# Staging tiles of a decoder trunk: six instead of four in the pair stages, moved to the right end of SBUF behind an empty margin

## The chip, the cores and the metric

The kernel runs on one core of a Trainium2 chip. The time is that of one execution on the device in microseconds; the profile is one further execution, taken by the hardware profiler.

## The reference

The reference is one layer of a hybrid decoder on 256 rows of width 4096, in float32. After an RMSNorm a wide projection W_in gives the inputs of two token mixers (gated linear attention with a per-channel decay; sliding-window attention with sinks) and of two merge gates. Each mixer's result is projected back to 4096 columns, both are merged by sigmoid gates, an output projection and a residual add follow, and a last RMSNorm:

```python
h = rms_norm(x, norm_gains[l])
z = h @ w_in[l]
...
y_a = (o_a * jax.nn.silu(gg)) @ w_gla_out[l]
...
y_b = (o_b * jax.nn.silu(sg)) @ w_swa_out[l]
merged = jax.nn.sigmoid(ga + b_gates[l, 0]) * y_a + jax.nn.sigmoid(gb + b_gates[l, 1]) * y_b
x = x + merged @ w_out[l]
return rms_norm(x, final_norm_gain)
```

## The kernel before

All matrix products keep float32 accuracy with a faster TensorE type: each operand is split into a high part (a cast to `fp32r` on ScalarE, L141) and a low part (what is left, a subtraction on VectorE, L142), and three matmuls (high x high, high x low, low x high) replace one. The activations lie in SBUF as the stationary operand (hT, then oaT, obT, mT, 65536 or 32768 bytes of a partition, on the left); the weights stream through as the moving operand, 512 columns at a time.

The weights come in staging tiles of 4096 bytes per partition, `raw`, loaded on SyncE's queue (L153, L206, L208). There are four, in one pool `stage` that lives through the whole kernel. From each staging tile `halves` makes a high and a low tile in the pool of the current phase: three of each in the phases of the mixers (STG), five in the pair phases (STM).

Two routines multiply:

- `gemm` (L145) makes one block of 256 rows by 512 columns: 16 loads, 192 matmuls. The mixers' 22 blocks are made this way, in the phases `hl0` (linear attention: blocks gq, gk, gv, gg) and `hl2` (window attention: sk, sv, sq, sg).
- `pair` (L186) makes two blocks at once. Per step j it takes two staging tiles (r, s). In an ordinary step, eight products of 128 x 128 x 512 are accumulated, 24 matmuls. In steps named by SEVEN (0, 2, 5 of 8, or 0, 3, 5, 8, 10, 13 of 16), seven products suffice, 21 matmuls: VectorE forms the sums t (L212), u (L213) and a new s (L214) of the weights, and four sets of halves are made instead of two. `outputs` (L247) then recombines the products from PSUM, through a tile `v`. The sums of the stationary operand that this needs, `xc`, are made once by `combine` (L165). The first pair of a stage has none yet and uses eight products everywhere.

Four stages are made of pairs: `ya` (phase `hl1`, four pairs of 8 steps, results put away in DRAM), `yb` (the same in phase `hl3`), the gates (ga0, gb0, ga1, ... gb3, eight pairs of 16 steps, each followed by a sigmoid and the product with `ya` or `yb`, read back in tiles `y` of 512 columns in a ring of two, `yr`), and `o` (four pairs of 16 steps, then residual and norm).

`combine` of hT for the gates is called behind the second pair of `yb` (argument `then`), so that all eight gate pairs use seven products.

Pools named by `phase` are stacked from the right end of SBUF. A pool that is opened where a closed one lay waits tile by tile (`reuse_waits="tile"`): the first writer of a new tile waits for the last readers of the old tiles beneath it.

The order of the instructions on each engine is worked out by the tile framework: it goes by program order, in which loads, sums and halves are pulled ahead (by 400 instructions in `gemm`, by 120 in `pair`), and by the time at which it expects operands and tiles to be ready. The queues then run in that order; a waiting instruction holds up what is behind it on its engine. SyncE's queue carries the weights in order, ScalarE's the casts and the loads of `y`, of the gate biases and of the residual.

Of the kernel before, what the change touches and what calls it, by code (L numbers as in the profile page):

```python
# [8 lines left out]
F32 = mybir.dt.float32  # L9
# [39 lines left out]
def trunk_kernel(  # L49
# [21 lines left out]
    big = ctx.enter_context(tc.tile_pool(name="big", bufs=1))  # L71
    stage = ctx.enter_context(tc.tile_pool(name="stage", bufs=4))
    dram = ctx.enter_context(tc.tile_pool(name="dram", bufs=1, space=bass.MemoryType.DRAM))
# [71 lines left out]
    def gemm(name, lhs, w, nkt, before=None, chunks=WHOLE):  # L145

        acc = [acc_ps.tile([P, NB], F32, tag="acc", name=f"{name}_a{t}") for t in range(NT)]
        for k0, n in [c for c in chunks if c[0] < nkt]:
            if before is not None:
                before(k0, n)  # L150
            with tc.high_priority(PRIO):
                raw = stage.tile([P, n, NB], F32, tag="raw", name=f"{name}_r{k0}")
                nc.sync.dma_start(raw, w[k0 // KW][:, k0 % KW : k0 % KW + n, :])  # L153
                hi, lo = halves(f"{name}_{k0}", raw, n)
            for t in range(NT):
                ts = slice(t * P, (t + 1) * P)
                for i in range(n):
                    kt = k0 + i
                    lh, ll = lhs[:, kt, 0, ts], lhs[:, kt, 1, ts]
                    nc.tensor.matmul(acc[t], lh, hi[:, i, :], start=kt == 0, stop=False)  # L160
                    nc.tensor.matmul(acc[t], lh, lo[:, i, :], start=False, stop=False)  # L161
                    nc.tensor.matmul(acc[t], ll, hi[:, i, :], start=False, stop=kt == nkt - 1)  # L162
        return acc

    def combine(lhs, xc, js, name):  # L165


        for c, j in enumerate(js):
            a = cur["hl"].tile([P, 2, NT, P], F32, tag="t2", name=f"{name}a{j}")
            nc.vector.tensor_tensor(  # L170
                a.rearrange("p k t c -> p k (t c)"), lhs[:, 2 * j : 2 * j + 2, 0, :].bitcast(F32),
                lhs[:, 2 * j : 2 * j + 2, 1, :].bitcast(F32), ALU.add,
            )
            d = cur["hl"].tile([P, 4, P], F32, tag="v", name=f"{name}d{j}")
# [5 lines left out]
            nc.vector.tensor_tensor(xc[:, c, :, 1, :], d, xc[:, c, :, 0, :].bitcast(F32), ALU.subtract)  # L180
# [5 lines left out]
    def pair(name, lhs, w, npr, xc=None, before=None, last=False):  # L186
# [14 lines left out]
        for j in range(npr):  # L201
            if before is not None:
                before(j)
            with tc.high_priority(PRM):
                r1 = stage.tile([P, 2, NB], F32, tag="raw", name=f"{name}_r{j}")
                nc.sync.dma_start(r1, w[j][:, 0:2, :])  # L206
                r2 = stage.tile([P, 2, NB], F32, tag="raw", name=f"{name}_s{j}")
                nc.sync.dma_start(r2, w[j][:, 2:4, :])  # L208
# [37 lines left out]

    def outputs(q, d, name):  # L247

        if 1 in q:
            v = cur["hl"].tile([P, NB], F32, tag="v", name=f"{name}_v")  # L250
            nc.scalar.copy(d[0][0], q[1])
            add(v, q[6], d[0][0])
            add(d[0][1], q[5], v, ALU.subtract)
            add(d[1][0], q[7], v)
            add(d[1][1], q[5], d[1][0], ALU.subtract)
# [5 lines left out]

    def spilled(name, lhs, w, dst, xc, pool, then=None):

        for n in range(NP2):
            q = pair(f"{name}{n}", lhs, w[n], OKT // 2, xc=None if n == 0 else xc)
            d = pool.tile([P, NT, 2, NB], F32, tag="ev", name=f"{name}_d{n}")
            outputs(q, [[d[:, t, i, :] for i in range(2)] for t in range(NT)], f"{name}{n}")
            for t in range(NT):
                nc.scalar.dma_start(dst[t][:, 2 * n * NB : 2 * (n + 1) * NB], d[:, t].rearrange("p i c -> p (i c)"))
            if n == 0:  # L270
                combine(lhs, xc, SEVEN[OKT // 2], name)
            if n == 1 and then is not None:
                then()

# [21 lines left out]
    with phase("hl0") as cur["hl"], phase("gla") as gp:  # L296
        cur["n"] = STG
        ssq = gp.tile([P, KW, S], F32, name="ssq")
# [13 lines left out]

        wd_raw = stage.tile([P, KT, RANK], F32, tag="raw", name="wd_raw")
        nc.sync.dma_start(wd_raw, wdec)
# [181 lines left out]
    with phase("hl1") as cur["hl"], phase("yap") as yp:  # L496
        cur["n"] = STM
        xca = yp.tile([P, len(SEVEN[OKT // 2]), 4, 2, P], F32R, name="xca")
# [3 lines left out]
    with phase("hl2") as cur["hl"], phase("swa") as sp:  # L502
        cur["n"] = STG
        mask = sp.tile([P, 3, P], F32, name="mask")
# [96 lines left out]

    cur["hl"], cur["n"] = ctx.enter_context(phase("hl3")), STM
    cur["n"] = STM
    xp = ctx.enter_context(phase("xp"))
    xch = xp.tile([P, len(SEVEN[KT // 2]), 4, 2, P], F32R, tag="xc", name="xch")
    with phase("ybp") as yp:
        xcb = yp.tile([P, len(SEVEN[OKT // 2]), 4, 2, P], F32R, name="xcb")
        spilled("yb", obT, wswa, yb_d, xcb, yp, lambda: combine(hT, xch, SEVEN[KT // 2], "h"))
    ep = ctx.enter_context(phase("ep"))


    m = big.tile([P, NT, DM], F32, tag="oT", name="m")
    for n in range(NP2):
        for w, (kind, y_d) in enumerate((("ga", ya_d), ("gb", yb_d))):
            cs = [slice((2 * n + i) * NB, (2 * n + i + 1) * NB) for i in range(2)]
            bt = ep.tile([P, 2, NB], F32, tag="bt", name=f"bt{w}{n}")
            nc.scalar.dma_start(bt, bgates[w, 2 * n * NB : 2 * (n + 1) * NB].partition_broadcast(P).rearrange("p (i c) -> p i c", i=2))
            q = pair(f"{kind}{n}", hT, wgate[w * NP2 + n], KT // 2, xc=xch)
            d = ep.tile([P, NT, 2, NB], F32, tag="ev", name=f"{kind}_d{n}")
            outputs(q, [[d[:, t, i, :] for i in range(2)] for t in range(NT)], f"{kind}{n}")  # L620
            for t in range(NT):
# [121 lines left out]
```

## Time and profile before

| | |
|---|---|
| median of 3 runs | 2614.85 us (2613.38 to 2619.92) |
| profiled execution | 2607.58 us |
| its span, first to last instruction | 2605.8 us |
| granted TensorE clock, mean | 0.989 |
| TensorE busy | 2503.3 us, 96% |
| VectorE busy | 1759.6 us, 68% |
| ScalarE busy | 1219.4 us, 47% |
| DMA, mean over the span | 188 GB/s |
| phases `hl0`, `ya`, `hl2` | 0 to 602, 602 to 783, 783 to 1294 us |
| `yb`, gates, `o` and the end | 1294 to 1488, 1488 to 2212, 2212 to 2606 us |

Rows of the profile name an engine (PE is TensorE, PEld its weight loads, DVE VectorE, ACT ScalarE, SP SyncE; a q behind it is its queue), a line of the kernel, and tiles as out<-in with the running numbers left out: `ga_t5l` is the low half of the sums t in step 5 of the four ga pairs. A row of waits reads: who waited <- for whom: us in total, times, longest. A row of the timeline begins with its start and its duration in us, and ends with the idle time of the engine before it, in brackets.

### The profile page before, as it was taken

To read this page: it belongs to the slowest core of one execution; us is meant where nothing else is said; L and a number is where in the kernel's file an instruction comes from. 1 tells how busy PE (TensorE), PEld (TensorE's weight loads), DVE (VectorE), ACT (ScalarE), POOL (GpSimd) and SP (SyncE) were. 2 spreads that over 40 slices of the span, in tenths; PEclk is the share of its full clock that TensorE was granted. 3 is DMA by queue.
4 is the path that set the end of the run, shared out by engine and by line. 5 is a ranking of instruction groups with operands and counts; after the bars stand their busy time and mean duration, and the time that the engine had idled before them with its cause. 6 is when DMAs were issued, how large, how long until landed. Compare 5 with 4: busy or idle time off the path is not lost.

```text
span 2605.8 us, 29359 instructions
## 1 busy us (share of the span) xinstructions
PE 2503.3 (96%) x10968; PEld 1996.1 (77%) x10968; DVE 1759.6 (68%) x1967; ACT 1219.4 (47%) x1488; POOL 41.9 (2%) x52
## 2 busy tenths in 40 slices
PE   8999999999999999999998999999999999999997
PEld 6778888887777888888786777777787777778765
DVE  7554555546774455555568778878878887857777
ACT  6444354434453344444544444445445445545444
POOL 4000000000000000000000000000000000000000
PEclk9999999999999999999998999999999999999999
DMA  7556556555666645555465666666666666555655
GB/s 254 150 172 187 166 178 185 170 169 166 222 202 202 186 151 175 159 148 184 130 201 163 205 214 203 194 217 198 200 201 207 206 199 220 184 179 193 217 190 190
DMA packets 139024, 491.14 MB, mean 188 GB/s; under 512 B 15840, under 2 KB 16224, under 8 KB 138880
## 3 DMA queue, kind: packets, MB, share of 16 engines
q1 hardware_dynamic: 127296, 461.69, 55.7%
q10 hardware_dynamic: 11584, 27.57, 3.1%
q8 instruction: 86, 1.41, 0.2%
q14 instruction: 58, 0.48, 0.1%
HBM read 476.61 MB, written 12.58 MB: 188 GB/s over the span
## 4 chain that ended last, share of the span: by engine, by line
PE 53%; DVE 24%; DMA 17%; issue 4%; ACT 1%; POOL 0%; ACTq 0%; SPq 0%; DVEq 0%; POOLq 0%
DMA ga_s<-in_wgate_dram 5%; DMA gb_s<-in_wgate_dram 4%; DMA o_s<-in_wout_dram 4%; PE sg_a L161 2%; PE gv_a L161 2%; PE sq_a L162 2%; PE sq_a L160 2%; PE gv_a L160 2%; PE sq_a L161 2%; PE gv_a L162 2%; PE sg_a L160 2%; PE sg_a L162 2%; PE gg_a L162 2%; PE gg_a L160 2%; PE gg_a L161 2%
## 5 line engine op out<-in xcount | busy, mean ns | idle before, releaser
L212 DVE TENSOR_TENSOR gb_t<-gb_r,gb_s 128x1024 f32<-128x1024 f32 x24 | 29.4, 1224 | 28.8 <-DMA gb_s<-in_wgate_dram 28.8
L212 DVE TENSOR_TENSOR ga_t<-ga_r,ga_s 128x1024 f32<-128x1024 f32 x24 | 29.4, 1224 | 24.0 <-DMA ga_s<-in_wgate_dram 24.0
L212 DVE TENSOR_TENSOR o_t<-o_r,o_s 128x1024 f32<-128x1024 f32 x18 | 22.0, 1225 | 32.4 <-DMA o_s<-in_wout_dram 32.3
L101 POOL TENSOR_TENSOR sf<-sf,mhalf 128x1 f32<-128x1 f32 x2 | 1.1, 550 | 1824.5 <-DVE sf L100 1824.5
L119 DVE SCALAR_TENSOR_TENSOR hT<-xsb,gin_sb,hT 128x256 fp32r<-128x256 f32 x32 | 26.1, 865 | 5.3 <-ACT hT L118 5.3
L565 ACT ACTIVATE s<-s,mx 128x128 f32<-128x128 f32 x64 | 28.4, 445 | 0.0
L128 POOL TENSOR_TENSOR ssq<-ssq,sq 128x512 f32<-128x512 f32 x15 | 25.6, 1709 | 24.5 <-ACT sq L127 23.9
L627 ACT ACTIVATE gb_d<-gb_d 128x512 f32<-128x512 f32 x16 | 10.1, 632 | 24.0 <-DVE gb_d L626 23.9
L212 DVE TENSOR_TENSOR ya_t<-ya_r,ya_s 128x1024 f32<-128x1024 f32 x9 | 11.0, 1225 | 14.5 <-DMA ya_s<-in_wgla_dram 14.4
L550 DVE SCALAR_TENSOR_TENSOR s<-s,mask 128x384 f32<-128x384 f32 x32 | 16.0, 552 | 6.0 <-PE s L549 6.0
L212 DVE TENSOR_TENSOR yb_t<-yb_r,yb_s 128x1024 f32<-128x1024 f32 x9 | 11.0, 1223 | 11.5 <-DMA yb_s<-in_wswa_dram 11.5
L656 ACT ACTIVATE xt<-x 128x512 f32<-128x512 f32 x16 | 10.0, 627 | 15.9 <-DVE x L245 15.9
L141 ACT CAST sg_16h<-sg_r 128x1024 fp32r<-128x1024 f32 x4 | 4.2, 1050 | 28.1 <-PE sg_a L162 28.1
L214 DVE TENSOR_TENSOR gb_s<-gb_u,gb_s 128x512 f32<-128x512 f32 x24 | 16.6, 690 | 0.5
L213 DVE TENSOR_TENSOR ga_u<-ga_t,ga_r 128x512 f32<-128x512 f32 x24 | 16.6, 690 | 0.5
L214 DVE TENSOR_TENSOR ga_s<-ga_u,ga_s 128x512 f32<-128x512 f32 x24 | 16.6, 690 | 0.5
L213 DVE TENSOR_TENSOR gb_u<-gb_t,gb_r 128x512 f32<-128x512 f32 x24 | 16.5, 688 | 0.4
L473 DVE COPY oraw<-op 128x512 f32<-128x512 f32 x8 | 5.5, 692 | 15.6 <-PE op L472 15.6
L118 ACT ACTIVATE hT<-xsb,gin_sb 128x256 fp32r<-128x256 f32 x32 | 14.0, 498 | 2.6 <-DMA xsb<-in_xT_dram 2.2
L582 DVE COPY pT<-pt 128x384 f32<-128x384 f32 x16 | 8.9, 555 | 9.3 <-PE pt L579 9.3
L141 ACT CAST gb_t10h<-gb_t 128x1024 fp32r<-128x1024 f32 x4 | 4.2, 1053 | 23.1 <-DVE gb_t L212 17.8
L579 PE MATMUL pt<-ident,s 128*128 128x128 f32 x96 | 15.0, 279 | 0.0
(2815 smaller groups left out, 9027.0 us busy)
## 6 DMA issues: line engine op xcount, KB each, us to landing
gv_r<-in_win_dram SPq DMA_DIRECT2D x64, 512.0 KB, 4.0
gg_r<-in_win_dram SPq DMA_DIRECT2D x64, 512.0 KB, 3.9
sq_r<-in_win_dram SPq DMA_DIRECT2D x64, 512.0 KB, 3.6
sg_r<-in_win_dram SPq DMA_DIRECT2D x64, 512.0 KB, 3.6
ga_r<-in_wgate_dram SPq DMA_DIRECT2D x64, 512.0 KB, 4.8
ga_s<-in_wgate_dram SPq DMA_DIRECT2D x64, 512.0 KB, 5.8
gb_r<-in_wgate_dram SPq DMA_DIRECT2D x64, 512.0 KB, 5.2
gb_s<-in_wgate_dram SPq DMA_DIRECT2D x64, 512.0 KB, 5.6
```

What stands on the lines that cost most here:

```text
L118: nc.scalar.activation(hT[:, kt, 0, :], xsb[:, kt, :], AF.Copy, scale=g)
L119: nc.vector.scalar_tensor_tensor(hT[:, kt, 1, :], xsb[:, kt, :], g, hT[:, kt, 0, :].bitcast(F32), ALU.mult, ALU.subtract)
L128: nc.gpsimd.tensor_tensor(ssq, ssq, sq, ALU.add)
L160: nc.tensor.matmul(acc[t], lh, hi[:, i, :], start=kt == 0, stop=False)
L161: nc.tensor.matmul(acc[t], lh, lo[:, i, :], start=False, stop=False)
L162: nc.tensor.matmul(acc[t], ll, hi[:, i, :], start=False, stop=kt == nkt - 1)
L212: nc.vector.tensor_tensor(ts, r1, r2[:, 0:1, :].broadcast_to([P, 2, NB]), ALU.add)
L213: nc.vector.tensor_tensor(t2[:, 0, :], ts[:, 1, :], r1[:, 0, :], ALU.add)
L214: nc.vector.tensor_tensor(r2[:, 0, :], t2[:, 0, :], r2[:, 1, :], ALU.add)
L550: nc.vector.scalar_tensor_tensor(s4[:, jj * 2 + half, :], sps[:, 0 : 3 * P], HD**-0.5, mask2, ALU.mult, ALU.add)
L565: nc.scalar.activation(s4[:, k, cs], s4[:, k, cs], AF.Exp, bias=mx[:, k, t : t + 1], accum_out=sm[:, k, t : t + 1],)
L579: nc.tensor.transpose(tp[:, m * P : (m + 1) * P], s4[:, k, m * P : (m + 1) * P], ident)
```

## The change

The staging tiles move from their own pool into the pool of the phase: four in `hl0` and `hl2` as before, six in `hl1` and `hl3`. At the very right end of SBUF an empty tile of 1152 bytes is put first, so that all pools of phases lie 1152 bytes further left.

Since the pools in the last phase then fill the space, several tiles are merged. The tile `v` goes into the ring `yr` of two (in `combine` its place is taken by `t13`). `xcb`, `xch` and `xcm` share one tile `xc`; the pool `ybp` is gone and `yb` uses the pool `ep` of the gates. `st` takes the place of `ev` at the end, and `sf` is a column of it. As `xch` can be written only when `xcb` is done with, `combine` of hT now comes behind the first gate pair, and this pair, ga0, uses eight products in every step.

```diff
+MARGIN = 1152
...
-    stage = ctx.enter_context(tc.tile_pool(name="stage", bufs=4))
...
+    ctx.enter_context(phase("margin")).tile([P, MARGIN // 4], F32, name="margin")
...
-                raw = stage.tile([P, n, NB], F32, tag="raw", name=f"{name}_r{k0}")
+                raw = cur["hl"].tile([P, n, NB], F32, tag="raw", name=f"{name}_r{k0}", bufs=cur["r"])
...
-            d = cur["hl"].tile([P, 4, P], F32, tag="v", name=f"{name}d{j}")
+            d = cur["hl"].tile([P, 4, P], F32, tag="t13", name=f"{name}d{j}")
...
-                r1 = stage.tile([P, 2, NB], F32, tag="raw", name=f"{name}_r{j}")
+                r1 = cur["hl"].tile([P, 2, NB], F32, tag="raw", name=f"{name}_r{j}", bufs=cur["r"])
...
-                r2 = stage.tile([P, 2, NB], F32, tag="raw", name=f"{name}_s{j}")
+                r2 = cur["hl"].tile([P, 2, NB], F32, tag="raw", name=f"{name}_s{j}", bufs=cur["r"])
...
-            v = cur["hl"].tile([P, NB], F32, tag="v", name=f"{name}_v")
+            v = pool.tile([P, NB], F32, tag="yr", name=f"{name}_v", bufs=2)
...
-            if n == 1 and then is not None:
-                then()
...
-        cur["n"] = STG
+        cur["n"], cur["r"] = STG, 4
...
-        cur["n"] = STM
+        cur["n"], cur["r"] = STM, 6
...
-    cur["hl"], cur["n"] = ctx.enter_context(phase("hl3")), STM
-    cur["n"] = STM
+    cur["hl"] = ctx.enter_context(phase("hl3"))
+    cur["n"], cur["r"] = STM, 6
     xp = ctx.enter_context(phase("xp"))
+    ep = ctx.enter_context(phase("ep"))
+    xcb = xp.tile([P, len(SEVEN[OKT // 2]), 4, 2, P], F32R, tag="xc", name="xcb")
+    spilled("yb", obT, wswa, yb_d, xcb, ep)
     xch = xp.tile([P, len(SEVEN[KT // 2]), 4, 2, P], F32R, tag="xc", name="xch")
-    with phase("ybp") as yp:
-        xcb = yp.tile([P, len(SEVEN[OKT // 2]), 4, 2, P], F32R, name="xcb")
-        spilled("yb", obT, wswa, yb_d, xcb, yp, lambda: combine(hT, xch, SEVEN[KT // 2], "h"))
-    ep = ctx.enter_context(phase("ep"))
...
-            q = pair(f"{kind}{n}", hT, wgate[w * NP2 + n], KT // 2, xc=xch)
+            q = pair(f"{kind}{n}", hT, wgate[w * NP2 + n], KT // 2, xc=None if n + w == 0 else xch)
+            if n + w == 0:
+                combine(hT, xch, SEVEN[KT // 2], "h")
...
-    st = ep.tile([P, NT, NBLK], F32, name="st")
+    st = ep.tile([P, NT, NBLK + 1], F32, tag="ev", name="st")
```

More of the change, by code (lines that the diff above doesn't have):

```diff
@@ L245, in add, with outputs @@
         nc.vector.tensor_tensor(o, a, b, op)
-    def outputs(q, d, name):
+    def outputs(q, d, name, pool):
         if 1 in q:
-            v = cur["hl"].tile([P, NB], F32, tag="v", name=f"{name}_v")
+            v = pool.tile([P, NB], F32, tag="yr", name=f"{name}_v", bufs=2)
             nc.scalar.copy(d[0][0], q[1])
@@ L260, in outputs, with spilled @@
                 nc.scalar.copy(d[t][i], q[b])
-    def spilled(name, lhs, w, dst, xc, pool, then=None):
+    def spilled(name, lhs, w, dst, xc, pool):
         for n in range(NP2):
@@ L266, in spilled @@
             d = pool.tile([P, NT, 2, NB], F32, tag="ev", name=f"{name}_d{n}")
-            outputs(q, [[d[:, t, i, :] for i in range(2)] for t in range(NT)], f"{name}{n}")
+            outputs(q, [[d[:, t, i, :] for i in range(2)] for t in range(NT)], f"{name}{n}", pool)
             for t in range(NT):
@@ L310, in trunk_kernel @@
         rms_scale(rstd, xps[:, 0:NT], DM)
-        wd_raw = stage.tile([P, KT, RANK], F32, tag="raw", name="wd_raw")
+        wd_raw = cur["hl"].tile([P, KT, RANK], F32, tag="raw", name="wd_raw", bufs=cur["r"])
         nc.sync.dma_start(wd_raw, wdec)
@@ L617, in trunk_kernel @@
             nc.scalar.dma_start(bt, bgates[w, 2 * n * NB : 2 * (n + 1) * NB].partition_broadcast(P).rearrange("p (i c) -> p i c", i=2))
-            q = pair(f"{kind}{n}", hT, wgate[w * NP2 + n], KT // 2, xc=xch)
+            q = pair(f"{kind}{n}", hT, wgate[w * NP2 + n], KT // 2, xc=None if n + w == 0 else xch)
+            if n + w == 0:
+                combine(hT, xch, SEVEN[KT // 2], "h")
             d = ep.tile([P, NT, 2, NB], F32, tag="ev", name=f"{kind}_d{n}")
-            outputs(q, [[d[:, t, i, :] for i in range(2)] for t in range(NT)], f"{kind}{n}")
+            outputs(q, [[d[:, t, i, :] for i in range(2)] for t in range(NT)], f"{kind}{n}", ep)
             for t in range(NT):
@@ L646, in trunk_kernel @@
         cs = [slice((2 * n + i) * NB, (2 * n + i + 1) * NB) for i in range(2)]
-        outputs(q, [[x2[:, t, cs[i]] for i in range(2)] for t in range(NT)], f"o{n}")
+        outputs(q, [[x2[:, t, cs[i]] for i in range(2)] for t in range(NT)], f"o{n}", ep)
         gf = ep.tile([P, 2, NB], F32, tag="bt", name=f"gf{n}")
@@ L658, in trunk_kernel @@
     for t in range(NT):
-        sf = ep.tile([P, 1], F32, name=f"sf{t}")
-        nc.vector.tensor_reduce(sf, st[:, t, :], AX.X, ALU.add)
+        sf = st[:, t, NBLK:]
+        nc.vector.tensor_reduce(sf, st[:, t, :NBLK], AX.X, ALU.add)
         rms_scale(sf, sf, DM)
```

2 lines of the change are left out of this document (1 added, 1 removed).

## The prediction, made before the change was run

> **What bounds the kernel now.** I read the page first: TensorE is busy for nearly the whole span, so only its gaps, its pace and its instruction count can move the time.
>
> ```profile
> span 2605.8 us, 29359 instructions
> PE 2503.3 (96%) x10968; PEld 1996.1 (77%) x10968; DVE 1759.6 (68%) x1967; ACT 1219.4 (47%) x1488; POOL 41.9 (2%) x52
> ```
>
> Busy PE is not PE at its peak, so next I took the pace. In PE's timeline over an undisturbed stretch of `gemm` the 50 matmuls from the first row to the second start 49 steps apart, 11.39 us: 0.2324 us each.
>
> ```profile
> 317.87 0.39 PE L161 MATMUL gq_a<-gq_4l,hT 128*128 128x512 f32 x1
> ...
> 329.26 0.39 PE L162 MATMUL gq_a<-gq_12h,hT 128*128 128x512 f32 x1
> ```
>
> Then the stages (busy time by stretch; PE, PEclk, DMA share, GB/s, and for the gate stage all engines). Each stage's loss is its length less its matmuls times 0.2324; the code gives 741 matmuls for `ya` and for `yb`, 366 for a seven-product gate pair, 384 for an eight-product one.
>
> ```profile
> 602.20:782.80 180.60, 176.15 (x741) 0.98 0.62 204
> 1294.10:1488.30 194.20, 178.16 (x742) 0.95 0.59 190
> 1488.30:1577.50 89.20, 86.49 (x368) 1.00 0.64 212
> 1488.30:2212.30 724.00, 696.79 (x2931) 549.94 (x2930) 583.46 (x629) 354.75 (x390) 0.00 (x0) 0.99 0.63 205
> ```
>
> `ya` loses 8.4 us (180.6 - 172.2), `yb` 22.0, the eight gate pairs 43.5 (724.0 - 2928 x 0.2324), the first of them 4.1. Who ends PE's waits there:
>
> ```profile
> PE yb_q L232 <- ACT yb_u0h L141: 12.7, 1, 12.7
> PE ga_q L233 <- DVE ga_t5l L142: 6.4, 4, 1.8
> ...
> PE gb_q L233 <- DVE gb_t5l L142: 5.2, 4, 1.4
> PE ya_q L233 <- DVE ya_s1l L142: 4.4, 2, 3.0
> ...
> PE ga_q L233 <- DVE ga_r4l L142: 4.0, 3, 1.3
> PE gb_q L233 <- DVE gb_r4l L142: 3.2, 4, 0.8
> PE o_q L233 <- DVE o_s4l L142: 3.1, 1, 3.1
> ...
> PE ga_q L232 <- DVE yb_d L245: 0.9, 1, 0.9
> ```
>
> PE waits for VectorE, which makes the low halves. VectorE in turn waits for weights to land, and their loads wait for one of four staging tiles to come free (waits of DVE, then of SyncE's queue):
>
> ```profile
> DVE o_t L212 <- DMA o_s<-in_wout_dram: 32.3, 15, 3.9
> DVE gb_t L212 <- DMA gb_s<-in_wgate_dram: 28.8, 20, 2.7
> DVE ga_t L212 <- DMA ga_s<-in_wgate_dram: 24.0, 17, 3.9
> ...
> SPq L206 <- DVE gb_r3l L142: 33.1, 4, 8.8
> ```
>
> So the chain is: slot free, load, VectorE, TensorE. Bandwidth does not bind: the gate stage moves 205 GB/s with the DMA engines 0.63 busy.
>
> **The change part by part.**
>
> *Two more staging tiles in the pair stages.* Nothing is added but lead: a load starts one j (two tiles) earlier. What this can give is limited by VectorE's own work. Its rows, in the order in which it runs them, with start to start in place of duration:
>
> ```profile
> 1683.14 1.23 DVE L212 TENSOR_TENSOR ga_t<-ga_r,ga_s 128x1024 f32<-128x1024 f32 x1 [0.20 <-DMA ga_s<-in_wgate_dram]
> 1684.29 0.68 DVE L245 TENSOR_TENSOR gb_d<-gb_d,ygb 128x512 f32<-128x512 f32 x1
> 1684.89 0.69 DVE L213 TENSOR_TENSOR ga_u<-ga_t,ga_r 128x512 f32<-128x512 f32 x1
> ```
>
> A 128x1024 operation takes 1.15 us, a 128x512 one 0.60. A seven-product j needs four of the first and three of the second, 6.4 us, against 21 x 0.2324 = 4.9 of PE; an eight-product j two of the first, 2.3, against 24 x 0.2324 = 5.6. A pair of 16 j (six of them seven-product) then needs 6 x 6.4 + 10 x 2.3 = 61.4, plus 8 x 0.60 = 4.8 for `outputs` and 5.2 (`ga`, 4 x 1.3) or 7.6 (`gb`, one more add each) for the gate arithmetic: 72.6 on the mean, which the gate row bears out (583.46 / 8 = 72.9). PE needs 85.1. But the work bunches: j 0, 3 and 5 are seven-product, and the previous pair's outputs and gates fall among them. Until the low half of `t5` VectorE owes 19.7 (j 0 to 4) + 4.8 + 3.5 (first half of j 5) + the gates, and it can be ahead by at most j 0 (6.4, the five high and low tiles are then full). PE arrives there after 26.5. While `gb` runs, `ga`'s 5.2 fall due: 19.7 + 4.8 + 3.5 + 5.2 - 6.4 = 26.8, so a stall of 0.3 remains of (5.2 + 3.2) / 4 = 2.1 now. While `ga` runs, `gb`'s 7.6, of which the last two operations (1.2) may come after `t5`: 28.0, so 1.5 remain of (6.4 + 4.0) / 4 = 2.6. In `o` there are two adds per quarter, 4.8: no stall remains.
>
> Stalls cost more than their length, because the clock drops behind some of them (PE windows around four of the stalls; the fourth number is the granted clock):
>
> ```profile
> 699.10:706.00 6.90, 3.88 (x11) 0.75 0.56 199
> 1385.00:1402.40 17.40, 4.57 (x12) 0.61 0.21 75
> 1692.00:1706.10 14.10, 10.93 (x40) 0.88 0.68 216
> ...
> 2336.00:2347.70 11.70, 8.26 (x28) 0.85 0.60 202
> ```
>
> The third window loses 14.1 - 40 x 0.2324 = 4.8 us for 3.2 of waiting, the first 4.3, the last 5.2. My estimates from these: `gb` pairs 4 x 1.8 = 7.2; `ga1` to `ga3` 3 x 1.1 of waiting and 3 more for the clock, together 6.3; `o` 12 (5.2 in the last window, its first seven-product pair, and 3.4 in each of the two others); `ya` and the rest of `yb` 6 (4.3 in the first window, the rest from the 1.4 left of `ya_s1l`). Sum -31.5; bounds 0 (VectorE's order decides alone) and -60 (all of it).
>
> *`combine` of hT, moved from behind `yb1` to behind `ga0`.* Its place now costs the window from 1385.0: 17.4 - 12 x 0.2324 = 14.6 us, where six combinations and `yb2`'s first sums share the tiles `t2` and `v`:
>
> ```profile
> L180 DVE TENSOR_TENSOR xch<-hd,xch x6: 681/693/693, 1382.9 to 1397.2; 128x512 fp32r<-128x512 f32 x6
> L180 DVE TENSOR_TENSOR xcm<-md,xcm x6: 684/684/686, 2243.2 to 2262.8; 128x512 fp32r<-128x512 f32 x6
> ```
>
> The second row is the same work on mT behind an eight-product pair: it ran inside `o0`, beside its matmuls. In the changed kernel hT's runs inside `ga0` in the same way; the shared `xc` tile is free by then, since `xcb`'s last reader is in `yb3`. I take -14.6; if `ga0` did not cover it, it would come back before `gb0`.
>
> *`ga0` with eight products.* 18 matmuls x 0.2324 = +4.2; its own loss of 4.1 should shrink by 2.6, as VectorE has only 37 us of halves there. Its first matmul, though, needs a bank that `yb3`'s last products fill: +1.0, by the 0.9 us wait for `yb_d` above, which is of this kind.
>
> *Staging moved into the phase pools.* At a phase's start a load must now wait for the old tiles beneath its slot. `ya`: the second slot lies under `oraw`, the fourth of `yb` under `on`, both read until just before the stage, while the tile that lands there is used half a step or more later; the others are free. `sk0` is worse: its four slots lie under `hl1`'s high tiles, the last of which PE reads until 782.8, so its second load starts there and lands 4.4 us later:
>
> ```profile
> sk_r<-in_win_dram SPq DMA_DIRECT2D x16, 512.0 KB, 4.4
> ```
>
> With a subtraction of 1.2 and a cast, taken as long, it is ready near 789.6, and PE wants it 12 matmuls into the block, at 785.6: 4.0 later, part of which stands where the first load's halves hold PE up today. I take +3 for all boundaries; bounds 0 and +9. SP's queue holds only these loads in order, so a late one holds up the next, but the next is due 2.8 us later.
>
> *`v` out of `t2`'s neighbour into the ring `yr`, `st` into `ev`.* No operation is added. `v` takes one of two slots from its writing to its second reader:
>
> ```profile
> L245 DVE TENSOR_TENSOR gb_d<-gb_q,gb_v x8: 681/682/686, 1664.3 to 2207.3; 128x512 f32<-128x512 f32 x8
> L245 DVE TENSOR_TENSOR gb_v<-gb_q,gb_d x4: 684/684/684, 1661.0 to 2203.8; 128x512 f32<-128x512 f32 x4
> ```
>
> That is 1661.0 to about 1665.6, 4.6 us. I cost it at nothing: the `y` behind it is wanted only at 1684.29 (the L245 row above).
>
> *The margin.* In the compiled kernel before, hT begins at byte 17248 of a partition, 864 into a row of 2048; the right end is at 229344, 2016 into a row, and so are the high and low tiles. With the margin all lie at 864. On VectorE addresses make no difference: the L212 operation on staging tiles takes 1.23 us and so does L142's on right-end tiles. On PE I take 0, with a rival below.
>
> Sum: -31.5 - 14.6 + 4.2 - 2.6 + 1.0 + 3.0 = -40.5. The profiled execution took 2607.6 us (span 2605.8), 7.3 below the median of the runs; the same step from the median, 2614.85, gives **2574**.
>
> **The rivals.** *The margin speeds up every matmul.* Matmuls whose weights are in `xc`, at the right end like the moving tiles, run faster than those with hT's:
>
> ```profile
> 1472.31 0.39 PE L232 MATMUL yb_q<-yb_t5h,xcb 128*128 128x512 f32 x1
> ...
> 1474.12 0.40 PE L234 MATMUL yb_q<-yb_u5h,xcb 128*128 128x512 f32 x1
> ```
>
> Nine in a row, 8 steps in 1.81 us: 0.226 against 0.2324. If lying alike is the reason, 4224 `gemm` matmuls gain 6 ns each, 25 us; of the pairs' 5910, all but 12 in each of 78 seven-product steps, 4974, gain up to 30, of which I count 15, as VectorE holds those stages. Time 2574 - 40 = 2534. Against it: these weights also differ from hT's in the end of SBUF, in the order of the products and in the PSUM banks they fill. [...]
>
> *VectorE's order binds, the lead gives nothing.* The bunching above holds and waits for DMA only turn into waits for free high and low tiles: -14.6 + 5.6 = -9, time 2606. Against it: DVE's 28.8 and 24.0 us of waiting lie just ahead of the stalls.
>
> *Slower: ScalarE stands at `y`'s issue.* The load of the second `y` (or `xt`) is issued on ScalarE's queue and now waits for `v`'s last reader. If it is placed too early, ScalarE's casts stand behind it, and PE and VectorE behind these: up to 4.6 us plus the clock loss, about 8, in each of ten seven-product pairs: 2574 + 80 = 2654; above 4 us per pair the change is a loss. Against it: with a ring of two, the third `y` waits for the first one's reader in the same way today.
>
> **How the numbers follow.** The forecast has 0.45, the margin 0.32, no gain from the lead 0.12, the stalled queue 0.11. The forecast's own range is 2550 to 2605 (bounds above). To hold 8 in 10 it reaches down over most of the margin's case: 2520 to 2608, leaving out the slower rival. A measurement tells about 0.3%, 7.8 us, from no change: forecast, margin and half of the third case are faster, 0.83; the other half is the same, 0.06; slower 0.11.
>
> **What would show it.** Right: DVE's waits at L212 for `ga_s`, `gb_s`, `o_s` below 25 us together (85 now); no 12.7 us wait in `yb`; `gb` pairs below 87.5 us; `xch`'s rows inside `ga0`; a new wait of about 2 us in `sk0`. The margin shows in the pace in `gemm`: 0.226 instead of 0.232 us. Wrong: waits of ScalarE's casts behind L625, or L212's waits gone and the `t5l` waits unchanged.

## The result and the profile after

| | before | after |
|---|---|---|
| median of 3 runs, us | 2614.85 (2613.38 to 2619.92) | 2492.58 (2492.32 to 2495.09) |
| ratio | 1 | 0.9531, 95% interval 0.9509 to 0.9553 |
| span of the profiled execution, us | 2605.8 | 2493.4 |

The kernel is 122 us faster, three times the 40.5 forecast, and 27 us below the end of the range. In the code after the change the lines lie two further down: the matmuls are L162 to L164 in `gemm` and L234 to L236 in `pair`, the casts L143, the low halves L144, the sums L214 to L216, the adds of `outputs` L247.

The page of the changed kernel has TensorE busy for 66 us less, with 18 matmuls more:

```profile
span 2493.4 us, 29365 instructions
PE 2437.6 (98%) x10986; PEld 1999.0 (80%) x10986; DVE 1724.6 (69%) x1929; ACT 1225.4 (49%) x1479; POOL 42.5 (2%) x52
```

So the pace itself has changed. PE's timeline in the same block `gq1` as before (start, duration); the two rows are 50 steps apart:

```profile
314.20 0.39 PE L162 MATMUL gq_a<-gq_4h,hT 128*128 128x512 f32 x1
...
325.53 0.39 PE L164 MATMUL gq_a<-gq_12h,hT 128*128 128x512 f32 x1
```

11.33 us / 50 = 0.2266 us a matmul, against 0.2324. The stages of the changed kernel (busy time by stretch: `ya`, `yb`, the first gate pair, the second, all eight, `o`):

```profile
597.02:773.20 176.18, 171.98 (x741) 139.93 (x741) 131.16 (x143) 84.17 (x90) 0.00 (x0) 0.99 0.61 206
1283.40:1460.10 176.70, 171.81 (x741) 139.85 (x741) 138.19 (x157) 88.98 (x96) 0.00 (x0) 0.99 0.68 222
1460.60:1548.00 87.40, 87.36 (x385) 72.37 (x386) 51.75 (x63) 36.65 (x39) 0.00 (x0) 1.00 0.62 196
1547.80:1630.90 83.10, 83.10 (x368) 68.83 (x367) 70.35 (x76) 45.93 (x51) 0.00 (x0) 1.00 0.69 219
1460.60:2128.90 668.30, 668.26 (x2948) 553.00 (x2949) 560.53 (x615) 354.65 (x383) 0.00 (x0) 1.00 0.69 220
2130.60:2479.30 348.70, 344.66 (x1531) 284.61 (x1530) 283.81 (x332) 183.48 (x220) 0.55 (x1) 0.99 0.62 199
```

In the gates, PE's busy time is now the whole length of the stretch: 366 x 0.2268 = 83.0 against 83.1 for a seven-product pair. There is no gap left to win there. What PE still waits for (a view of waits, as before):

```profile
PE yb_q L234 <- DVE yb_d L247: 4.1, 2, 2.5
PE yb_q L234 <- ACT yb_r0h L143: 3.9, 1, 3.9
PE ya_q L234 <- ACT ya_r0h L143: 3.9, 1, 3.9
...
PE ya_q L234 <- DVE ya_d L247: 3.4, 2, 2.0
...
PE sk_a L162 <- ACT sk_0h L143: 2.3, 1, 2.3
```

The `t5l` and `r4l` rows of the gates and the 12.7 us for `yb_u0h` are gone. In their place stand waits at the starts of `ya`, `sk0` and `yb` (1.0, 1.4 and 1.3 us before), and two for PSUM banks (`ya_d`, `yb_d`) that the kernel before did not have at this length. VectorE's waits for weights at the sums t of the gates and `o` have fallen from 85 us to 25:

```profile
DVE gb_t L214 <- DMA gb_s<-in_wgate_dram: 11.0, 5, 2.6
...
DVE o_t L214 <- DMA o_s<-in_wout_dram: 9.1, 5, 3.3
```

(and 4.7 for `ga_s`).

### The profile page after: what moved, and what is told of

Its sections match the earlier page's. It is cut to its first block, busy times and chain, and to the rows that moved or that the text cites. A ratio compares the mean times of both kernels' runs of the same rounds, so it can differ in the third digit from the quotient of the medians.

```text
span 2493.4 us, 29365 instructions
## 1 busy us (share of the span) xinstructions
PE 2437.6 (98%) x10986; PEld 1999.0 (80%) x10986; DVE 1724.6 (69%) x1929; ACT 1225.4 (49%) x1479; POOL 42.5 (2%) x52
## 4 chain that ended last, share of the span: by engine, by line
PE 89%; DVE 5%; issue 2%; DMA 2%; ACT 1%; POOL 0%; SPq 0%; ACTq 0%; POOLq 0%; DVEq 0%
PE ga_q L234 5%; PE ga_q L236 4%; PE ga_q L235 4%; PE gb_q L236 4%; PE gb_q L234 4%; PE gb_q L235 4%; PE o_q L236 4%; PE o_q L235 4%; PE o_q L234 4%; PE sg_a L163 2%; PE sg_a L162 2%; PE sq_a L164 2%; PE sq_a L163 2%; PE sq_a L162 2%; PE sg_a L164 2%; PE gg_a L164 2%
## 5 line engine op out<-in xcount | busy, mean ns | idle before, releaser
L214 DVE TENSOR_TENSOR gb_t<-gb_r,gb_s 128x1024 f32<-128x1024 f32 x24 | 29.3, 1221 | 11.0 <-DMA gb_s<-in_wgate_dram 11.0
L214 DVE TENSOR_TENSOR o_t<-o_r,o_s 128x1024 f32<-128x1024 f32 x18 | 22.0, 1221 | 9.1 <-DMA o_s<-in_wout_dram 9.1
L214 DVE TENSOR_TENSOR ga_t<-ga_r,ga_s 128x1024 f32<-128x1024 f32 x18 | 22.0, 1221 | 4.9 <-DMA ga_s<-in_wgate_dram 4.7
L143 ACT CAST sg_16h<-sg_r 128x1024 fp32r<-128x1024 f32 x4 | 4.2, 1056 | 28.0 <-PE sg_a L164 28.0
L214 DVE TENSOR_TENSOR ya_t<-ya_r,ya_s 128x1024 f32<-128x1024 f32 x9 | 11.0, 1222 | 8.6 <-DMA ya_s<-in_wgla_dram 8.6
L214 DVE TENSOR_TENSOR yb_t<-yb_r,yb_s 128x1024 f32<-128x1024 f32 x9 | 11.0, 1222 | 8.4 <-DMA yb_s<-in_wswa_dram 8.4
L216 DVE TENSOR_TENSOR gb_s<-gb_u,gb_s 128x512 f32<-128x512 f32 x24 | 16.5, 688 | 0.3
L464 POOL TENSOR_SCALAR_AFFINE_SELECT ats<-ats 128x128 f32<-128x128 f32 x16 | 8.0, 523 | 415.4 <-DVE ats L462 415.4
L476 ACT ACTIVATE jk<-oraw 128x256 f32<-128x256 f32 x16 | 6.7, 418 | 16.9 <-DVE oraw L473 16.6
L579 PEld LDWEIGHTS pt<-ident,s 128*128 128x128 f32 x96 | 11.4, 145 | 4.4 <-ACT s L565 3.9
L288 PE MATMUL m_t<-ident,m 128*128 128x128 f32 x64 | 10.2, 302 | 3.7 <-DVE mT L279 3.7
```

Source lines behind the costliest of these rows:

```text
L214: nc.vector.tensor_tensor(ts, r1, r2[:, 0:1, :].broadcast_to([P, 2, NB]), ALU.add)
L579: nc.tensor.transpose(tp[:, m * P : (m + 1) * P], s4[:, k, m * P : (m + 1) * P], ident)
```

## The experiments

Ratios are to the kernel before, run on the same chip, with 95% intervals; the medians of the kernel before on those chips were 2610 to 2611 us. On the changed kernel's own chip it was 2614.85, from three runs, so differences from the changed kernel come out some 5 us smaller by medians than by ratios; where it matters both are given.

### Four corners: staging tiles and margin

The corners are four or six staging tiles, each with and without the margin.

**e1: the change without its margin.**

```diff
-    ctx.enter_context(phase("margin")).tile([P, MARGIN // 4], F32, name="margin")
```

> The changed kernel without its empty 1152 bytes: all tiles of the right end lie 1152 bytes higher, at 2016 into a row of 2048 as before, nothing else is changed. Theory (the margin sets the matmul pace): gemm and pair matmuls start every 232.4 ns again instead of 226.8; 9198 matmuls with weights from hT, mT, oaT or obT x 5.6 ns = 52 us, so 2545 us. Rival 1 (the pace has another cause in the change, the order or the pools): the pace stays at 226.8 ns and the time at 2493. Rival 2 (part of the pairs is held by VectorE, which then hides a slower TensorE): only gemm loses, 4224 x 5.6 ns = 24 us, 2517.

2538.9 us, 0.9728 (0.9713 to 0.9744). `gemm` and pairs run at 232 ns again. The loss against the changed kernel is 0.0197 or 51 us by the ratios, 46 by the medians, 42 by the spans of the two profiled executions (2535.0 and 2493.4), where the theory has 52. In the traces the pair stages lose 26 of the theory's 28 us, so hardly any of it is hidden by VectorE: with six tiles the gate pairs have no gaps at the slower pace either. The phases of the mixers lose 16 of 24; why not all stays open.

**e2: the kernel before with the margin alone.**

```diff
+    ctx.enter_context(phase("margin")).tile([P, 1152 // 4], F32, name="margin")
```

> The kernel before with the empty 1152 bytes alone: four staging tiles, combine of hT behind yb1. Theory: gemm pace 226.8 ns, 24 us; the pairs' pace falls too, but the waits for VectorE take back about half of their 28 us: 2614.9 - 24 - 14 = 2577; 2563 if nothing is taken back. Rival (the pace is not the margin's): 232.4 ns and 2615.

2591.3 us, 0.9923 (0.9903 to 0.9943): 20 us. The pace fell to 226.8, but only the phases of `gemm` gain by it. The gate stage and `o` of this kernel, by stretch:

```profile
1470.10:2197.20 727.10, 689.60 (x2931) 547.11 (x2930) 579.71 (x625) 351.79 (x388) 0.00 (x0) 0.99 0.63 203
2201.50:2579.50 378.00, 354.75 (x1530) 284.68 (x1530) 284.44 (x333) 179.91 (x220) 0.55 (x1) 0.98 0.59 187
```

PE is busy for 7 us less in the gates than before (689.60 against 696.79), and the stage is no shorter: 727.1 against 724.0. With four tiles the pairs run at the pace of the loads and VectorE; a faster matmul only lengthens the gaps (`ya`, `yb` and `o` are no shorter either: 183.4, 194.8 and 378.0 us against 180.8, 194.3 and 376.4). All of the pairs' 28 us was taken back, where half was expected.

**e3: the change with four tiles.**

```diff
-        cur["n"], cur["r"] = STM, 6
+        cur["n"], cur["r"] = STM, 4
```

(in `hl1` and in `hl3`)

> The changed kernel with four staging tiles in place of six in the pair stages (ya, yb, gates, o); margin and the moved combine stay. Theory (the lead removes the waits for VectorE): the waits for t5l, r4l, s4l come back, with the 31 us that the prediction gave to the lead: 2524, and up to 2540 because TensorE is now faster and VectorE is not. Rival (the faster pace or the moved combine removed the stalls): 2493, no t5l waits. In both the gemm pace stays at 226.8 ns.

2589.4 us, 0.9924 (0.9907 to 0.9941). The waits are back, as the theory has it,

```profile
PE ga_q L235 <- DVE ga_t5l L144: 5.7, 3, 1.9
...
PE ga_q L235 <- DVE ga_r4l L144: 4.0, 3, 1.3
...
PE o_q L235 <- DVE o_s4l L144: 3.0, 1, 3.0
```

but four tiles cost 97 to 103 us (against the changed kernel's median, and by the ratios), three times the sum expected.

**e11: four tiles and no margin**, both edits at once.

> The changed kernel with four staging tiles in the pair stages and without the empty 1152 bytes: the fourth corner beside e1 (six, none: 0.9728 of the kernel before), e3 (four, 1152: 0.9924) and the changed kernel (six, 1152: 0.9531). What is left of the change is the moved combine, the staging in the pools of the stages and v in yr. Theory (with four tiles the loads hold VectorE and the pair stages whatever TensorE's pace, so the margin is worth only gemm's 20 us there, and the lead alone is worth about 65 without the margin): 2589 + 20 = 2609, 0.999 of the kernel before. Rival (margin and lead add up without touching each other: 0.9924 + 0.9728 - 0.9531 = 1.0121): 2641.

2612.0 us, 1.0001 (0.9988 to 1.0015). The four corners in one table:

| | four tiles | six tiles | lead |
|---|---|---|---|
| no margin | 1.0001 | 0.9728 | -0.0273, 71 us |
| margin 1152 | 0.9924 | 0.9531 | -0.0393, 103 us |
| margin | -0.0077, 20 us | -0.0197, 51 us | |

The two do not add up: by themselves they give 20 and 71 us, together 123. That leaves 32 by the ratios, 24 by the medians and 20 by the traced spans, for which both are needed. It is about the pairs' share of the pace (28 by the theory, 26 in the traces of e1 and the changed kernel), which pays only when the pairs no longer wait. And without lead and margin, the rest of the change is worth nothing.

**e4: the moved `combine` alone.**

```diff
-        spilled("yb", obT, wswa, yb_d, xcb, yp, lambda: combine(hT, xch, SEVEN[KT // 2], "h"))
+        spilled("yb", obT, wswa, yb_d, xcb, yp)
...
-            q = pair(f"{kind}{n}", hT, wgate[w * NP2 + n], KT // 2, xc=xch)
+            q = pair(f"{kind}{n}", hT, wgate[w * NP2 + n], KT // 2, xc=None if n + w == 0 else xch)
+            if n + w == 0:
+                combine(hT, xch, SEVEN[KT // 2], "h")
```

> The kernel before with combine of hT behind ga0 and ga0 with eight products, alone. Theory (the prediction's terms): -14.6 in yb, +4.2 for 18 matmuls, -2.6 of ga0's own loss, +1.0 for the bank: 2614.9 - 12.0 = 2603. Rival (the combine only moves its cost, since with four staging tiles VectorE falls behind in ga0 or gb0 as well): 2615.

2602.4 us, 0.997 (0.9954 to 0.9987): 8 us, by the interval 3 to 12, where 12 were expected. In its trace `yb` shortens from 194.3 to 182.0 us and `ga0` lengthens from 89.2 to 91.8 by the first and the last matmul of each; a wait of 3.7 us for `yb_d` at the start of `ga0` takes a further part, which leaves 6.0:

```profile
PE ga_q L232 <- DVE yb_d L245: 3.7, 1, 3.7
```

From e4 to e11 (staging in the pools of the stages, `v` in `yr` and the other merged tiles, not separated here) the ratio rises by 0.0031, 8 us. The two cancel.

### Where the operands lie

**e5: matmuls alone, by the places of weights and moving tiles.** No other engine works beside them.

```diff
+    for s, (a, b) in enumerate(SEGS):
+        q = ps.tile([P, NB], F32, tag="q", name=f"s{s}w{a}m{b}")
+        wo, mo = at(BASE, a), at(BASE + 8192, b)
+        for g in range(NG):
+            ...
+            nc.tensor.matmul(q, lh, hi, start=g == 0, stop=False)
+            nc.tensor.matmul(q, lh, lo, start=False, stop=False)
+            nc.tensor.matmul(q, ll, hi, start=False, stop=g == NG - 1)
```

> Only matmuls are left of the kernel (the output is not the reference's): 36 streams of 72 matmuls in gemm's order (lh with hi, lh with lo, ll with hi), each stream with one place of the weights and one of the moving tiles within a row of 2048 bytes, nothing beside them. Theory (lying alike decides, relative to each other): weights at 864 give 226.8 ns a matmul with moving tiles at 864 and 232.4 with 2016, whichever stands first; weights at 2016 give 226.8 with 2016 and 232.4 with 864; equal places are fast wherever they lie. Open: whether alike within 512 bytes (864 and 352, 1376, 1888) is enough: if only a row of 2048 counts these give 232.4. Rival 1 (the place of the moving tiles alone decides: 864 is good, 2016 bad): weights at 2016 with moving at 2016 give 232.4. Rival 2 (it takes the kernel's other engines, places are nothing to TensorE): one pace everywhere.

Four streams in PE's timeline, first and last matmul of each. They have the weights at 864 and the moving tiles at 2016 (`s1`) and 864 (`s2`), then the weights at 2016 and the moving tiles at 2016 (`s15`) and 864 (`s16`):

```profile
34.33 0.40 PE L45 MATMUL s1w864m<-m,w 128*128 128x512 f32 x1
...
50.89 0.39 PE L47 MATMUL s1w864m<-m,w 128*128 128x512 f32 x1
51.12 0.39 PE L45 MATMUL s2w864m<-m,w 128*128 128x512 f32 x1
...
67.22 0.39 PE L47 MATMUL s2w864m<-m,w 128*128 128x512 f32 x1
...
266.46 0.39 PE L45 MATMUL s15w2016m<-m,w 128*128 128x512 f32 x1
...
282.56 0.39 PE L47 MATMUL s15w2016m<-m,w 128*128 128x512 f32 x1
282.78 0.40 PE L45 MATMUL s16w2016m<-m,w 128*128 128x512 f32 x1
...
299.34 0.39 PE L47 MATMUL s16w2016m<-m,w 128*128 128x512 f32 x1
```

Each has 71 steps: 16.56 / 71 = 0.2332 us, 16.10 / 71 = 0.2268, 0.2268 and 0.2332. So it is the distance that decides, not the place. The mean step over the later two thirds of each stream, for weights at 864, by distance of the moving tiles:

```
distance, bytes   ns a matmul
0                 226.7
32                233.3
64                228.8
128               232.5
192               233.3
256               226.7
320               228.9
384               232.2
448               233.4
512               226.7
640               233.4
1024, 1536        226.7
1152              233.4 and 232.2 (two streams)
```

Every multiple of 256 that was tried is fast, 226.7 ns in the table, with weights at 0, 32, 64, 96 and 2016 too where it was tried. At 160 within 256 (weights at 96, 352 and 864) it is 234.2 to 234.3. At a distance of 128 within 256, that of the kernel before, a stream settles at 232.2 to 232.5 or at 233.4. The open question is answered: alike within 256 bytes is enough at the distances tried (256, 512, 1024 and 1536 bytes, 226.7 ns each), as long as all matmuls of a stream have the same distance (e9 has streams in which they do not).

**e8: the change with a margin of 128 bytes.**

```diff
-MARGIN = 1152
+MARGIN = 128
```

> The changed kernel with an empty 128 bytes at the right end in place of 1152: the moving tiles lie at 1888 into a row of 2048, the weights of the left end at 864, so 1024 apart, alike within 256 bytes and not within 2048. Theory (from the streams: distances of 256, 512, 1024 and 1536 bytes gave 226.7 ns like distance 0, so only the place within 256 bytes counts): 226.8 ns a matmul and 0.953 of the kernel before, 2493 us. Rival (in the whole kernel the row of 2048 counts, as the change's words have it): 232.4 ns and 0.973, 2545 us.

2492.5 us, 0.9552 (0.9534 to 0.957), and 50 steps in `gk0` take 11.33 us, as with 1152:

```profile
61.72 0.39 PE L162 MATMUL gk_a<-gk_0h,hT 128*128 128x512 f32 x1
...
73.05 0.39 PE L164 MATMUL gk_a<-gk_8h,hT 128*128 128x512 f32 x1
```

That is 0.2266 us a matmul with weights and moving tiles 1024 bytes apart. The rows of 2048 bytes, by which the prediction gives the places, are a way of counting and play no part here; 1024 bytes of the margin are not needed. The weights of one matmul are 128 columns of hT, which by the code begin at 864 or a multiple of 512 bytes further, so within 256 bytes all matmuls on hT have the same distance, 128 before the change and 0 after it.

**e9: what collides.** The same streams with other sizes, the distance 0 or 128 bytes.

```diff
+    ("c384alike", ((A, A),), P, 384), ("c384off", ((A, B),), P, 384),
+    ("c256alike", ((A, A),), P, 256), ("c256off", ((A, B),), P, 256),
+    ("w64alike", ((A, A),), 64, 512), ("w64off", ((A, B),), 64, 512),
...
+    ("own_alike", ((A, A), (B, B)), P, 512), ("next_alike", ((A, B), (B, A)), P, 512),
```

> Only streams of 72 matmuls again (the output is not the reference's), moving tiles 0 or 128 bytes from the weights' place, with fewer moving columns (384, 256), with fewer weight columns (64, 32), and two streams that alternate between two places 128 bytes apart: in one each matmul's weights lie like its own moving tile and unlike its neighbours', in the other unlike its own and like its neighbours'. Theory (while a moving tile streams, the weights of the next matmul are read; the two reads meet when they lie unlike): the loss of 5.8 to 6.7 ns is a price per load of weights, so it stays about the same with 384 and 256 moving columns and shrinks with 64 and 32 weight columns; the stream that is alike with its neighbours is fast (226.7), the one alike with its own is slow (232 to 234). Rival (the matmul compares its own two operands): the reverse for the last two streams, and a loss in proportion to the moving columns, half at 256.

```
stream                                       alike    128 off   (ns a matmul)
128 weight columns, 512 moving               226.7    233.4
128 weight columns, 384 moving               173.3    176.1
128 weight columns, 256 moving               120.0    118.6
64 weight columns, 512 moving                230.1    229.4
32 weight columns, 512 moving                231.7    230.8
alternating, alike with its own tile         228.4
alternating, alike with its neighbours'      230.0
```

Both theories fall. The loss is neither a price per load of weights (at 256 columns it is gone, 118.6 against 120.0 ns) nor one per column (it would be half), and with narrower weights the streams that lie alike are slow as well (230.1 and 231.7). Nor is it enough that each matmul lies alike with itself: the stream that alternates between two places takes 228.4. How the places act on each other stays open: the two reads that meet and the matmul that compares its own operands were guesses, and no trace shows either. Shown is only that for 128 x 128 weights and 512 columns, where all matmuls of a stream share one distance, that distance within 256 bytes decides: 226.7 ns alike, 228.8 to 234.3 at the others tried.

The streams also set `fp32r` beside float32. In the kernel before, the float32 products of 128 x 128 weights and 256 columns at L471 and L472 take 0.43 us each from start to start (166.11, 166.54, and the next at 166.97 us), with PE busy throughout; in `fp32r` here it is 120.0 ns alike.

### The lead, and the starts of the stages

**e6: five staging tiles.**

```diff
-        cur["n"], cur["r"] = STM, 6
+        cur["n"], cur["r"] = STM, 5
```

> The changed kernel with five staging tiles in place of six. With four it took 0.9924 of the kernel before, with six 0.9531, so the lead is worth 103 us in the changed kernel. Theory (each tile of lead lets VectorE run further ahead, until it covers the bunch of three seven-product steps): five give more than half of it, since the longest wait goes first: 2615 x 0.965 = 2523. Rival (loads come in pairs of two tiles, so a fifth tile lets no whole step start earlier): at most a quarter, 2570.

2497.8 us, 0.9554 (0.9524 to 0.9583). The fifth tile brings 0.0370 of the 0.0393, more than the theory asked. The sixth is worth 0.0023, less than the intervals can tell (that of the changed kernel is 0.9509 to 0.9553). In the traces it removes the last waits in the gates, which with five still show,

```profile
PE ga_q L235 <- DVE ga_t5l L144: 5.7, 3, 1.9
```

(681.4 us for the eight pairs against 668.3), but it makes `ya` and `yb` longer: 176.2 and 176.7 us, against 170.5 and 170.1 with five. VectorE's timeline in the changed kernel shows why, with six tiles:

```profile
679.12 0.69 DVE L247 TENSOR_TENSOR ya_v<-ya_q,ya_d 128x512 f32<-128x512 f32 x1
682.14 1.23 DVE L214 TENSOR_TENSOR ya_t<-ya_r,ya_s 128x1024 f32<-128x1024 f32 x1 [2.33 <-DMA ya_s<-in_wgla_dram]
...
685.02 0.68 DVE L247 TENSOR_TENSOR ya_d<-ya_q,ya_v 128x512 f32<-128x512 f32 x1
```

The sums of step 2 (L214) stand in VectorE's program among the adds of `outputs`, wait 2.33 us for their load, and PE waits behind them for the banks (`ya_d`, 2.0 us the longest).

**e7: four tiles that stay, two more.**

```diff
+    def raw_tile(shape, name):
+        i = cur["i"] % cur["r"]
+        cur["i"] += 1
+        if i < 4:
+            return stage.tile(shape, F32, tag="raw", name=name)
+        return cur["hl"].tile(shape, F32, tag="raw", name=name, bufs=cur["r"] - 4)
...
+        cur["n"], cur["r"], cur["i"] = STM, 6, 0
```

> The changed kernel, with four of the six staging tiles in a pool that stays for the whole kernel, as before, and only the other two in the pools of the pair stages; the ring of six begins with the four that stay. Theory (the dearer starts of ya, sk0 and yb come from first loads that wait for the old tiles beneath their places): the waits of 3.9 us at ya_r0h and yb_r0h and of 2.3 us at sk_0h fall by 3, 2.3 and 3 us: 8 us, 2493 - 8 = 2485. Rival (these starts are dearer because TensorE arrives earlier than before, and VectorE and ScalarE are still busy with the stage that ends): no difference, 2493.

2479.9 us, 0.9492 (0.9471 to 0.9513). This interval overlaps a little with the changed kernel's (0.9509 to 0.9553), not with that of e8 (0.9534 to 0.957), which is the changed kernel at the same pace. The waits at the starts of `ya`, `sk0` and `yb` fall from 3.9, 2.3 and 3.9 us to these (the code is eight lines longer here; the `sk0` one is now for the low half):

```profile
PE sk_a L171 <- DVE sk_0l L152: 1.5, 1, 1.5
PE ya_q L242 <- ACT ya_r0h L151: 1.3, 1, 1.3
PE yb_q L242 <- ACT yb_r0h L151: 1.0, 1, 1.0
```

The span is 15 us shorter than the changed kernel's. The starts of `ya`, `sk0` and `yb` account for 3.2, 2.4 and 2.9 of it, the block `sk0` for 2.1 and the first block for 2.0. The theory holds for the starts: the first loads were their cause. The 2.0 of the first block may be chance: it took from 54.6 us (e3) to 56.5 (e6) in kernels that are the same up to there.

**e10: the same with five tiles in `ya` and `yb`.**

```diff
-        cur["n"], cur["r"], cur["i"] = STM, 6, 0
+        cur["n"], cur["r"], cur["i"] = STM, 5, 0
...
+    cur["r"], cur["i"] = 6, 0
```

(the first edit in `hl1` and in `hl3`, the last line ahead of the gates; the phase's pool keeps two slots, which take turns as the fifth tile)

> The kernel of e7 (four staging tiles that stay, two more in the pair stages) with a ring of five instead of six in ya and yb only. In e6 ya and yb took 170.5 and 170.1 us with five tiles, in the changed kernel 176.2 and 176.7 with six, where VectorE's sums for a later step stand in its program ahead of the outputs, wait for their load, and TensorE waits for the banks (ya_d, yb_d). Theory: 5 us less in each of ya and yb than in e7, 2480 - 10 = 2470, 0.9453 of the kernel before, with no wait for ya_d or yb_d left. Rival (with the tiles that stay the order comes out otherwise, or the first gate pair starts later): 2480.

2473.3 us, 0.948 (0.9462 to 0.9497); the interval lies below the changed kernel's. Against e7 the two intervals overlap, but the traces agree with the theory: `ya` takes 171.2 us and `yb` 170.6, 4.3 and 4.8 less, and no wait for `ya_d` is left, nor one for `yb_d` within `yb`. A wait for `yb_d` at the first gate pair, 0.5 us in e7, gives part of it back, as the rival said of the first gate pair; the span is 8 us shorter than in e7.

```profile
PE ga_q L242 <- DVE yb_d L255: 2.8, 1, 2.8
```

## Why the prediction was wrong, and where it was right

Step by step, from ratios of neighbouring kernels (e4, e11, e1, the changed kernel) times 2615:

| term | predicted | measured |
|---|---|---|
| `combine` of hT with `ga0` and its bank | -12.0 | -8 |
| staging in the pools of the stages, `v` | +3, bounds 0 and +9 | +8 |
| two more staging tiles | -31.5, bounds 0 and -60 | -71 |
| margin | 0, rival -40 | -51 |
| sum | -40.5 | -123 |

As lead and margin act on each other, their split depends on the order: with the margin first it is -20 and -103. By the medians the margin's -51 is -46.

**The step that failed first: the margin was taken at 0.** The rows that spoke for it were in the prediction (0.226 us with `xc`, 0.2324 with hT), and its reading, lying alike, was right. What was said against it was given more weight than the two paces. No run shows the 0: it was the author's choice, and the runs gave -20 us with four tiles (e2) and -51 with six (e1 against the changed kernel). In e5, with nothing beside PE, the distance of its two operands alone moves the pace from 226.7 to 233.4 ns. None of the other differences that were held against the rival (the end of SBUF, the order of the products, the PSUM banks) is needed: in e5 all tiles lie at one end, the order is the same and the banks take turns, and the pace still follows the distance. The rival also was too small: it let VectorE take back half of the pairs' gain. In e2 all of it is taken back, and with six tiles next to nothing (26 of 28 us stay), since there the gate pairs wait for nothing. The sum adds up terms that act on each other.

**The second: VectorE's bill for the lead.** It found VectorE's work until `t5l` to be 26.8 to 28.0 us after a pair's start, PE's arrival at 26.5, and so left stalls of 0.3 to 1.5 us. The bill put all eight operations of `outputs` behind the start, and let two of the twelve gate operations of `gb` follow `t5l`. VectorE's timeline in e1, same pace as before, six tiles:

```profile
1649.43 0.69 DVE L245 TENSOR_TENSOR gb_v<-gb_q,gb_d 128x512 f32<-128x512 f32 x1
1650.15 1.29 DVE L245 TENSOR_TENSOR gb_d<-gb_q,gb_v 128x512 f32<-128x512 f32 x2
...
1652.48 0.69 DVE L245 TENSOR_TENSOR gb_d<-gb_q,gb_d 128x512 f32<-128x512 f32 x1
1653.40 0.69 DVE L245 TENSOR_TENSOR gb_d<-gb_q,gb_d 128x512 f32<-128x512 f32 x1 [0.23 <-PE gb_q L234]
1654.00 1.22 DVE L142 TENSOR_TENSOR ga_s0l<-ga_s,ga_s0h 128x1024 fp32r<-128x1024 f32 x1
1655.14 1.28 DVE L245 TENSOR_TENSOR gb_d<-gb_q,gb_d 128x512 f32<-128x512 f32 x2
...
1680.51 1.22 DVE L142 TENSOR_TENSOR ga_t5l<-ga_t,ga_t5h 128x1024 fp32r<-128x1024 f32 x1
```

and PE's, with the pair's first matmul and its first on `t5l`:

```profile
1655.28 0.39 PE L232 MATMUL ga_q<-ga_t0h,xch 128*128 128x512 f32 x1
...
1682.15 0.39 PE L233 MATMUL ga_q<-ga_t5l,xch 128*128 128x512 f32 x1
```

Five of the eight run before the pair starts, since four banks are complete with the last seven-product step, long before the pair's end, and all of step 0's halves are ready too. All gate operations run ahead of `t5l`. The bill is then 19.7 + 3 x 0.60 + 3.5 + 7.6 - 6.4 = 26.2, and `t5l` is done at 1681.73, 26.45 after the start, 0.4 before PE wants it. At the faster pace it is closer still (the changed kernel, VectorE's row and PE's):

```profile
1655.70 1.22 DVE L144 TENSOR_TENSOR ga_t5l<-ga_t,ga_t5h 128x1024 fp32r<-128x1024 f32 x1
```

```profile
1657.06 0.41 PE L235 MATMUL ga_q<-ga_t5l,xch 128*128 128x512 f32 x1
```

Done at 1656.92, wanted at 1657.06. So VectorE is close to being the next bound of the gates, but it does not bind yet.

**The third: what a removed stall is worth.** The prediction had the whole loss of the gates in hand (43.5 us) and priced only the two listed waits of each pair and the clock behind them, 13.5, with 2.6 in `ga0` some 16. With no stall left, all of it goes. The gates and `o` with four tiles (e11) and with six (e1), at one pace and with the same number of matmuls:

```profile
1492.20:2220.70 728.50, 701.62 (x2948) 552.28 (x2949) 560.65 (x613) 346.85 (x382) 0.00 (x0) 1.00 0.63 200
2224.90:2595.00 370.10, 356.95 (x1530) 284.49 (x1530) 283.85 (x329) 179.82 (x219) 0.00 (x0) 0.99 0.60 189
```

```profile
1481.20:2164.20 683.00, 683.00 (x2948) 555.44 (x2949) 562.01 (x615) 354.02 (x383) 0.00 (x0) 1.00 0.69 215
2165.90:2521.00 355.10, 350.91 (x1531) 284.83 (x1530) 284.77 (x332) 182.95 (x221) 0.55 (x1) 1.00 0.62 195
```

The gates gain 45.5 us by the lead; from the kernel before, with 18 matmuls more, it is 724.0 + 4.2 - 683.0 = 45.2. In `ga1` of the kernel before, what steps longer than 0.26 us take beyond the pace adds up to 7.8 us, which is the whole loss of the pair; the two listed waits hold 3.5 of them, `s0h` 1.0, and the rest are shorter ones, steps lengthened by 0.1 to 0.3, and the low clock behind `t5l`, of which the prediction counted only a part. In `o` the lead gains 15.0, where 12 were taken, and in `ya` and `yb` together 8.0, where 6 were. So most of the shortfall of the lead is in the gates. (`o` had 376.4 us in the kernel before; the 6.3 that are gone with four tiles already, in e11, belong to the rest of the change; why stays open.)

**Right**: bandwidth did not bind (205 GB/s in the gates before, 220 after, with the DMA engines 0.63 and 0.69 busy); the chain of slot, load, VectorE and TensorE was the bound (e3, e6, e11); `combine` in `yb` cost about what was said (12.3 us gone, of 14.6). `ga0` with eight products lengthened by 2.6 where 4.2 - 2.6 = 1.6 were taken, and its bank cost 3.7 in e4 where 1.0 was taken, which makes 6 of the 12 in that trace and 8 by the ratio. The term for the staging stayed within its bounds by luck as well: in the traces of e4 and e11 the starts alone come to 9.0, `ya` is 3.8 longer besides, and `o` 7.4 shorter. The starts are `sk0` with 2.4, its wait of 2.3 as forecast, and `ya` and `yb` with 2.9 and 3.7, which the prediction had put at nearly nothing, since it took only the second slot of `ya` and the fourth of `yb` to be covered. The slower rival did not come: ScalarE's longest waits in the gates are casts that wait for the sums, not for the loads of `y`, and PE is busy throughout.

```profile
ACT ga_t8h L143 <- DVE ga_t L214: 13.8, 3, 5.0
ACT gb_t8h L143 <- DVE gb_t L214: 11.1, 4, 2.8
```

Of the signs named beforehand all those of the forecast came true (24.8 us of DMA waits, no 12.7 us wait, `gb` pairs of 83.1 us, 2.3 us at `sk0`), `xch` was made within `ga0` (from 1460.6) but for the first of its six parts,

```profile
L182 DVE TENSOR_TENSOR xch<-hd,xch x6: 684/684/694, 1455.1 to 1479.8; 128x512 fp32r<-128x512 f32 x6
```

and the margin's sign, 0.226 us, came true as well. Where the lead is concerned the forecast had the mechanism and missed the size; with the margin it missed the effect itself.

## What to carry to other kernels

Where a stage has gaps, take its loss as length less matmuls times pace, not as the sum of its listed waits: a remedy that removes the last of the waits can bring the whole loss, as it did in the gates. Two edits can each be small alone and large together, when one speeds an engine that the other stops from waiting; test the corners. If two groups of the same matmuls run at different paces, lay the operands alike and measure it before an argument is found against it; here 128 bytes were worth 42 to 51 us beside six tiles, and 20 beside four. A buffer that outlives the stages keeps its loads ahead across a stage's start (waits of 1.3, 1.5 and 1.0 us at `ya`, `sk0` and `yb` in e7, where the changed kernel has 3.9, 2.3 and 3.9); two more in the stage's pool gave the lead without that price.

## What the hardware showed that was not expected

- In a stream of `fp32r` matmuls of 128 x 128 weights and 512 columns with one distance throughout, a matmul starts every 226.7 ns when moving tile and weights lie at the same place within 256 bytes, and every 228.8 to 234.3 ns at the other distances tried (e5), with no other engine at work.
- This does not carry to all sizes: with 384 columns the streams still take 173.3 ns alike and 176.1 at 128 bytes, but with 256 columns 120.0 and 118.6, with 64 weight columns 230.1 and 229.4 (e9). Narrower weights are not faster: 230.1 ns alike with 64 columns and 231.7 with 32, against 226.7 with 128.
- At a distance of 128 bytes a stream has two paces, 232.2 to 232.5 and 233.4 ns, both seen in e5 for the same places; which it falls into was not settled.
